# Moving one gate group, turning the first block's outputs on VectorE, and tying the stores of x to products

## The chip, the cores and the metric

The kernel runs on one NeuronCore of one Trainium2 chip. The metric is the device time of one execution in microseconds (us). Three executions of the kernel before took 2559.28, 2559.40 and 2559.43 us; their median is 2559.4 us. The trace comes from one more execution, which was recorded by the profiler.

## What is computed

The reference is one layer that mixes a short convolution (path A) with a chunked linear recurrence of eight heads (path B), for 2048 prompt tokens and 64 sample tokens, of width 1024:

```
h = rms_norm(x, g_pre);  vA, bA, cA, zA, q, f, iv, zB, gA, gB = split(h @ w_in)
yA = (silu(zA) * bA * conv3(cA * vA)) @ w_a_out
o  = hgrn2(q, k, v, logf)              # per head; chunks of 64 tokens, state 128x128
o  = o * rsqrt(mean(o*o) + eps)        # per head and token
o  = o * g_onorm
yB = (o * silu(zB)) @ w_b_out
merged = sigmoid(gA) * yA + sigmoid(gB) * yB
x  = x + rms_norm(merged @ w_o, g_post)
gate = sigmoid(rms_norm(x, g_ple) @ w_ple_gate)
x  = x + (p @ w_ple_proj) * gate
```

## The kernel before

**Layout.** Features lie on the 128 partitions and tokens along the free dimension. The 2112 tokens are cut into three blocks of 768, 704 and 640 tokens (`SIZES`, L36). Each block goes through path B's heads (`path_b`, L1213), path A (`path_a`, L880), the merge of both with the output projection (`in_turn`, L558), and a last stage with the final norm and the final gate (`final_norm` L1405, `final_gate` L1458).

**Products.** Each fp32 operand is split into a high part, which is rounded, and a low part, which is what rounding took away (`split`, L225: ScalarE writes the high part, VectorE the low one). A product is three passes, high by high, high by low and low by high (L442 to L444). Two column blocks of the weights and two halves of the block's tokens are taken together in `sgroup` (L427), which needs seven products instead of eight by adding and subtracting operands. I call this a group. One product of a group is 12 matmuls. The sums of the weights that a group needs (S1 to S4) and their low parts are made in the first block by VectorE and stored to DRAM (`keep_sum` L328, `split_w` L263); in later blocks they are loaded (L274, L236). Where a group was not done in the first block, its first run in a later block makes and stores the sums (`combined`, L341, with `first or i1 not in sums`). These stores go through the queue in `stores[0]`: SyncE's (SP) in the first block, GpSimd's (POOL) after it.

**Order of the work.** The kernel is written for a scheduler which orders each engine's instructions by dependencies and by the order of the program. `hook()` (L313) runs at the end of every product of a group and takes one entry of the list `hooks`; so side work is spread over products: one entry is one slot. `paced` (L300) adds a dependency of a DMA on the last matmul that was emitted so far (`last[0]`): the DMA is sent only when that matmul is done. `behind_all` and `tc.issue_after` only fix an order on an engine.

**Heads.** `head_prep` (L936) runs two groups for a head: f with v, then z with q (`sink_q`, L1019). The first block puts z through SiLU on ScalarE (L1023); the other blocks take a sigmoid (L1026) and multiply by v and by g_onorm on VectorE (L1027). `head_attn` (L1068) is the attention of a head over up to four pairs of chunks. Its last steps norm the output `on` (L1184) and then turn it, from tokens on partitions to features on partitions, so that it can be multiplied into z. In the first block TensorE turns it: six 128x128 transposes for each head (L1189), and VectorE multiplies the PSUM result by g_onorm and z (L1193, two instructions). In the other two blocks the pairs of chunks are turned in another way: VectorE transposes 32x32 blocks (`turned`, L1049, L1053), POOL stores the result to DRAM (`to`, L1055) and reads it back in another order (`in_rows`, L1057, L1060), and VectorE multiplies it into z (`scale_o`, L1209, L1211). Only the single chunk of 64 tokens that is left over goes through TensorE there (L1195). The finished z of each head is stored by POOL (`keep_z`, L1216, L1218).

**Gate groups.** The gates gA and gB are 16 column blocks, so 8 groups (`gates`, L868). The first block runs seven of them, one after each of heads 1 to 7. For the other two blocks `LEAD` = 7 groups run ahead, under the final norm of the block before (main loop); the eighth, columns 6 and 7 of gB, runs in `path_b` after the `head_prep` of head 5 (L1223, `hd == KH + 1`), with `stores[0]` set to SP meanwhile. The first block never makes the sums of this group, so the middle block makes them.

**The stores of x.** In the first two blocks the eight tiles of the new x (`xo`) are stored to DRAM in the last part of `final_norm` (L1447), and read back in `final_gate`. `fetch` (L1414) loads the eight tiles of the old x there. `final_norm` runs in hooks of the seven gate groups; in its last part, one step comes with every second product.

Of the kernel before, what the change touches and what calls it, by code (L numbers as in the profile page):

```python
# [14 lines left out]
ALU = mybir.AluOpType  # L15
# [3 lines left out]
P = 128  # L19
D = 1024  # L20
KB = D // P
KH = KB // 2
NH = 8
# [70 lines left out]
def hybrid_step(  # L94
# [17 lines left out]
    V, A, G, T, SP = nc.vector, nc.scalar, nc.gpsimd, nc.tensor, nc.sync  # L112
# [13 lines left out]
    def nm(s):  # L126
        uid[0] += 1
        return f"{s}_{uid[0]}"
# [38 lines left out]
    def spill(kind, j):  # L167
        return dram.tile([P, BN], F32, tag=f"{kind}{j}", name=nm(kind), bufs=2)[:, : width[0]]
# [13 lines left out]
    g_pre, g_on, g_post, g_ple = (vec[:, i, :] for i in range(4))  # L182
    cw = [vec[:, 4 + i, :] for i in range(3)]
    caus = [const.tile([P, P], I32, tag=f"caus{i}", name=f"caus{i}") for i in range(2)]
    keep = const.tile([P, BN], F32, tag="keep", name="keep")
# [53 lines left out]
    lows, turn, stores = {}, [0], [SP]  # L239
# [54 lines left out]
    last, hooks, copies, adds, ahead, evicted, freed, powers, means = [None], [], [None], [None], [], [], [], [], []  # L294
# [5 lines left out]
    def paced(dma):  # L300

        tc.add_manual_dep(
            dma.ins, last[0].name, mybir.DependencyInfo(mybir.DependencyClass.Sync, mybir.DependencyReason.DATA), reason="paced"
        )
# [170 lines left out]
    def half(t, h):  # L475
        return t[:, h * hn() : (h + 1) * hn()]

    def whole(x, y):

        if y is None:  # L480
            return x
        t = hf()
        freed[:] = [V.tensor_tensor(t, x, y, ALU.add).ins]
        return t
# [451 lines left out]
    def head_prep(bl, hc, hd, first, hs, before):  # L936
        n, npair = bl["n"], bl["npair"]
# [29 lines left out]
        ka, kb, qe, z = hf(npair * CH), rt(), rt(), rt()  # L967
# [51 lines left out]
        def sink_q(c, h, x, y):  # L1019
            if c == 1:  # L1020
                into(half(qe, h), x, y)
            elif first:
                A.activation(half(z, h), whole(x, y), AF.Silu)  # L1023
            else:
                v = whole(x, y)
                A.activation(half(z, h), v, AF.Sigmoid)  # L1026
                V.scalar_tensor_tensor(half(z, h), v, g_on[:, hd : hd + 1], half(z, h), ALU.mult, ALU.mult)  # L1027
# [4 lines left out]
            queries()  # L1032
        with behind_all([*wrote, *powers]):
            by_token = [in_rows("tv", npair)]
            if before is not None and before["on"] is not None:
                before["ot"] = in_rows("to", npair, before["on"])
            if not first:
                by_token.insert(0, in_rows("tk", npair))
# [29 lines left out]
    def head_attn(ip, gs, d, hd):  # L1068
# [3 lines left out]
        nt, ln = len(gs), gs[0]["len"]  # L1072
        o0, n = gs[0]["off"], nt * ln
        qe, z, att = d["qe"], d["z"], atts[ip]
        single = ln < P
# [26 lines left out]
        with placed():  # L1102
            for i, g in enumerate(gs):
                o = g["off"]
                shared = nt == 2 * SWAP
                if not single and (i < SWAP or not shared):
                    at = (d["more"] + 2 * i if shared else (o - SWAP * 2 * P) // P) * CH
# [26 lines left out]
        for i, g in enumerate(gs):  # L1134
            u = p_u[:, i * P : i * P + P]
            c = (g["off"] + ln) // CH - 1
# [25 lines left out]
        with placed():  # L1162
            for i, g in enumerate(gs):
                dst = p_o[:, i * P : i * P + P]
                T.matmul(dst, att[:, i, :], v[:, i], start=True, stop=prevs[i] is None)  # L1165
                if prevs[i] is not None:
                    T.matmul(dst, cols(d["qx"], g), prevs[i], start=False, stop=True)  # L1167
        if not d["first"] and not single:
            d["on"] = rt(d["npair"] * P) if d["on"] is None else d["on"]
            on = cols3(d["on"][:, o0:], nt)  # L1170
        else:
            on = tile3(2)
# [13 lines left out]
        p_t = ps_attn()  # L1186
# [1 line left out]
            for i in range(nt):  # L1188
                T.transpose(p_t[:, i * P : i * P + P], on[:, i, :], ident)  # L1189
        c = slice(o0, o0 + n)  # L1190
        turned_o = p_t[:, P - ln : P - ln + n]
        if d["first"]:
            V.scalar_tensor_tensor(z[:, c], turned_o, g_on[:, hd : hd + 1], z[:, c], ALU.mult, ALU.mult)  # L1193
        else:
            V.tensor_tensor(z[:, c], turned_o, z[:, c], ALU.mult)  # L1195
        yield

    def each(steps):
# [7 lines left out]
        if "ot" not in d:  # L1206
            d["ot"] = in_rows("to", d["npair"], d["on"])

    def scale_o(d, hd):  # L1209
        z = d["z"][:, : d["npair"] * P].rearrange("q (g i a) -> q g i a", i=4, a=32)  # L1210
        V.tensor_tensor(z, d["ot"], z, ALU.mult)  # L1211

    def path_b(bl, hc, first, kept, fills, hs, lead_sums=None):  # L1213


        def keep_z(hd, z):  # L1216
            kept["o", hd] = spill("o", hd)
            G.dma_start(kept["o", hd], z)  # L1218

        slots, base, d = {}, 0, None  # L1220
        for hd in range(NH):
            d = head_prep(bl, hc, hd, first, hs, d)
            if hd > 0 if first else hd == KH + 1:  # L1223
                queue, stores[0] = stores[0], SP
                next(fills, None)
                stores[0] = queue
            assert not hooks
            attn = [head_attn(i, gs, d, hd) for i, gs in enumerate(bl["parts"])]
            keep = partial(keep_z, hd, d["z"])
            piece = lead_sums and partial(next, lead_sums, None)  # L1230

            def at(slot, *steps):
                slots.setdefault(base + slot, []).extend(s if callable(s) else partial(next, s) for s in steps if s is not None)

            if first:
                late = int(hd == 0)
                for g in attn:
                    for slot in (1 + late, 4, 7, 10, 13):
                        at(slot + late + (g is attn[1]), g)
                at(15 + late, keep)  # L1240
                for slot in (15, 17, 19) if hd else (17,):
                    at(slot, piece)
                if hd == NH - 1:
                    for slot in range(22, 70, 4):
                        at(slot, piece)
            else:
                pairs, one = attn[:2], attn[2:]
                for slot, steps in enumerate((pairs[:1], pairs[1:], one, one, pairs, one, pairs, (), one)):
                    at(slot + 2, *steps)
                at(11, partial(turn_o, d))  # L1250
                at(14, partial(read_o, d))
                at(14 + 7, partial(scale_o, d, hd), keep)
            count = 14 + 7 * (first or hd + 1 == KH + 1) if hd + 1 < NH else 1 + max(slots) - base
            for slot in range(base, base + count):
                steps = slots.pop(slot, None)
                hooks.append(partial(each, steps) if steps else None)
            base += count
# [147 lines left out]
    def final_norm(bl, segs, xo, acc, h2, kept, ask_ahead=False):  # L1405

        c = slice(segs[0]["off"], segs[-1]["off"] + hn())
        n = len(segs) * hn()  # L1410
        acc2, rs, rs2 = rt(), rt(), rt()
        xks = []

        def fetch():  # L1414
            j = len(xks)
            if j < KB:
                xks.append(rt())
                G.dma_start(xks[j][:, c], x_fm[j * P : (j + 1) * P, segs[0]["t0"] : segs[0]["t0"] + n])

        for _ in range(2 if bl["last"] else 4):  # L1420
            fetch()
        if kept is not None:
            for j in range(KB):
                sum_squares(j, xo[j], acc, width[0])
                if j % 2:
                    yield
        yield from rms(acc, rs, segs, bl["last"])
        if ask_ahead:
            for _ in range(3):
                fetch()  # L1430
                fetch()
                yield
        for j in range(KB):
            fetch()
            xj = xo[j][:, c]
            V.scalar_tensor_tensor(xj, xj, g_post[:, j : j + 1], rs[:, c], ALU.mult, ALU.mult)
            V.tensor_tensor(xj, xj, xks[j][:, c], ALU.add)

            for i in (j,) if not bl["last"] else (j - 1,) if 0 < j < KB - 1 else (j - 1, j) if j else ():
                sum_squares(i, xo[i][:, c], acc2[:, c], n)  # L1440
            yield
        yield from rms(acc2, rs2, segs, bl["last"])
        ts = []
        for j in range(KB):
            if kept is not None:
                kept["x", j] = spill("x", j)
                G.dma_start(kept["x", j], xo[j])  # L1447
            if len(h2) <= j:
                h2.append((rt(dt=F32R), rt(dt=F32R)))

            for i in (j, j + 1) if j == 0 else (j + 1,):
                if i < KB:
                    ts.append(rt())
                    V.scalar_tensor_tensor(ts[i][:, c], xo[i][:, c], g_ple[:, i : i + 1], rs2[:, c], ALU.mult, ALU.mult)
            split(ts[j][:, c], h2[j][0][:, c], h2[j][1][:, c])
            yield
# [178 lines left out]
    fills = sized(blocks[0], gates(blocks[0], hc, kepts[0], True))  # L1635
    for bi, bl in enumerate(blocks):
        first, kept = bi == 0, kepts[bi]
# [26 lines left out]
        mg, xo, h2, acc = [], [], [], rt()  # L1664
# [17 lines left out]
        before, loads, ob, m = merge_in_turn(a, kept, mg, first)  # L1682
# [31 lines left out]
        if nxt:  # L1714
            xo.extend(stages[-1]["mid"])
            fills = sized(nxt, gates(nxt, hc, kepts[bi + 1], False))
# [65 lines left out]
```

## Time and profile before

| | |
|---|---|
| median of three executions | 2559.4 us |
| the profiled execution's own time | 2566.42 us |
| its span, first to last instruction | 2564.2 us |
| mean granted TensorE clock | 0.997 |
| TensorE matmul / weight load busy | 2533.4 / 2516.8 us |
| VectorE / ScalarE / POOL busy | 1795.1 / 1481.9 / 448.1 us |
| moved by DMA | 774.70 MB, mean 302 GB/s |

The profiled execution took 7.0 us more than the median. In the rows of the profile PE is TensorE, PEld its weight loads, DVE VectorE, ACT ScalarE, SP SyncE. A row of a group names the line, engine and operation, then output and inputs by the program's tile names with their sizes, how often (x), and after the bar the busy time and the mean ns of one, then the idle time ahead of it. A row of a window gives, for each engine, the busy us and in brackets how many instructions, then the granted TensorE clock as a share of full speed (PEclk), the busy share of the 16 DMA engines, and GB/s. Matmuls overlap, so the duration in their rows is longer than the distance from one to the next; the distance is what counts. A row of the timeline gives start, duration, instruction, and in square brackets the idle time ahead of it with what ended it.

### The profile page before, as it was taken

Reading aid. Unit: us, or ns where it says so; the run is one execution under the profiler, and the core shown is the slowest. Engines: PE = TensorE matmul, PEld = TensorE weight load, DVE = VectorE, ACT = ScalarE, POOL = GpSimd, SP = SyncE. Lnnn points to the kernel's source line nnn. Section 1 sums busy time; section 2 is a strip of 40 time slices with the busy share of each in tenths; the row PEclk is TensorE's granted clock in tenths of the full one; section 3 lists DMA queues with packets and bytes.
Section 4 is the critical chain, followed back from the end, with each engine's and each line's share of the span. In section 5 each row is a group of like instructions: output and inputs, shape, how many; then the busy total and the mean of one; then the engine's idle time right before and its main releaser. Section 6 shows DMA issues by size and latency. Waiting matters only on the chain. (4 is left out here: it accounts for less than half of the span.)

```text
span 2564.2 us, 47005 instructions
## 1 busy us (share of the span) xinstructions
PE 2533.4 (99%) x16070; PEld 2516.8 (98%) x16070; DVE 1795.1 (70%) x3549; ACT 1481.9 (58%) x2876; POOL 448.1 (17%) x793
## 2 busy tenths in 40 slices
PE   9999999999999999999999999999999999999999
PEld 9999999999999999999899999999999999999998
DVE  7888888898868775577574556887437766336967
ACT  6666666554453664466464555666446665446675
POOL 2011121230022021122122221102112221001011
PEclk9999999999999999999999999999999999999999
DMA  8789888998797888888888998998889999989986
GB/s 329 245 283 318 276 291 289 323 367 302 255 342 252 269 306 270 302 275 293 283 276 308 338 389 311 337 303 315 306 302 319 326 328 321 302 300 324 336 273 202
DMA packets 370399, 774.70 MB, mean 302 GB/s; under 512 B 45734, under 2 KB 50528, under 8 KB 370160
## 3 DMA queue, kind: packets, MB, share of 16 engines
q1 hardware_dynamic: 321840, 582.95, 66.8%
q0 software_dynamic: 48320, 188.75, 20.6%
q8 instruction: 126, 2.06, 0.3%
q14 instruction: 113, 0.93, 0.1%
HBM read 559.43 MB, written 212.10 MB: 301 GB/s over the span
## 5 line engine op out<-in xcount | busy, mean ns | idle before, releaser
L442 PE MATMUL pg<-r,hi 128*128 128x320 f32 (+2 forms) x3304 | 1082.3, 328 | 1.7 <-ACT hf L456 1.4
L443 PE MATMUL pg<-r,hi 128*128 128x320 f32 (+2 forms) x3304 | 1067.7, 323 | 0.0
L444 PE MATMUL pg<-r,lo 128*128 128x384 f32 (+2 forms) x2368 | 773.3, 327 | 10.6 <-DMA lo<-low 9.7
L273 ACT CAST hi<-raw 128x512 fp32r<-128x512 f32 x726 | 447.1, 619 | 498.4 <-PE pg L443 172.4
L442 PEld LDWEIGHTS pg<-r,hi 128*128 128x128 f32 x3304 | 623.4, 189 | 2.9 <-ACT hf L456 2.2
L443 PEld LDWEIGHTS pg<-r,hi 128*128 128x128 f32 x3304 | 623.1, 189 | 0.0
L444 PEld LDWEIGHTS pg<-r,lo 128*128 128x128 f32 x2368 | 445.6, 188 | 12.8 <-DMA lo<-low 11.5
L444 PE MATMUL pg<-r,s 128*128 128x320 f32 (+1 forms) x936 | 296.6, 317 | 3.0 <-DMA s<-low 3.0
L594 PE MATMUL pg<-r,hi 128*128 128x320 f32 (+2 forms) x864 | 277.2, 322 | 0.5 <-DVE r L226 0.4
L593 PE MATMUL pg<-r,hi 128*128 128x320 f32 (+2 forms) x864 | 274.9, 322 | 0.0
L226 ACT CAST hi<-raw 128x512 fp32r<-128x512 f32 x252 | 155.3, 620 | 157.8 <-PE pg L443 42.7
L226 DVE TENSOR_TENSOR r<-r,r 128x320 fp32r<-128x320 f32 (+7 forms) x350 | 206.3, 609 | 45.7 <-ACT r L226 44.2
L226 DVE TENSOR_TENSOR lo<-raw,hi 128x512 fp32r<-128x512 f32 x231 | 158.1, 687 | 80.5 <-ACT hi L226 76.3
L226 ACT CAST r<-r 128x320 fp32r<-128x320 f32 (+7 forms) x350 | 183.1, 556 | 43.8 <-DVE r L1333 8.4
L595 PE MATMUL pg<-r,lo 128*128 128x352 f32 (+2 forms) x564 | 181.0, 321 | 1.3 <-DMA lo<-low 1.2
L444 PEld LDWEIGHTS pg<-r,s 128*128 128x128 f32 x936 | 176.3, 188 | 4.0 <-DMA s<-low 3.9
L226 ACT CAST hi<-s 128x512 fp32r<-128x512 f32 x160 | 98.8, 618 | 137.6 <-PE pg L443 109.8
L632 PE MATMUL pg<-r,hi 128*128 128x384 f32 (+2 forms) x512 | 167.0, 327 | 0.2 <-DVE r L226 0.2
L631 PE MATMUL pg<-r,hi 128*128 128x384 f32 (+2 forms) x512 | 165.6, 327 | 0.2 <-ACT hi L273 0.2
L594 PEld LDWEIGHTS pg<-r,hi 128*128 128x128 f32 x864 | 162.2, 188 | 2.1 <-DVE r L226 1.6
L593 PEld LDWEIGHTS pg<-r,hi 128*128 128x128 f32 x864 | 161.2, 188 | 1.3 <-ACT r L226 0.8
L456 ACT COPY hf<-pg 128x352 f32<-128x352 f32 (+2 forms) x354 | 157.4, 446 | 2.6 <-PE pg L444 2.1
(394 smaller groups left out, 4109.6 us busy)
## 6 DMA issues: line engine op xcount, KB each, us to landing
raw<-w_blk SPq DMA_DIRECT2D x578, 256.0 KB, 4.4
raw<-S SPq DMA_DIRECT2D x440, 256.0 KB, 4.7
lo<-low SPq DMA_DIRECT2D x421, 256.0 KB, 4.4
s<-low SPq DMA_DIRECT2D x305, 256.0 KB, 4.6
low<-lo SPq DMA_DIRECT2D x275, 256.0 KB, 4.1
S<-s SPq DMA_DIRECT2D x156, 256.0 KB, 3.9
low<-r POOLq DMA_DIRECT2D x50, 256.0 KB, 5.2
r<-w_blk POOLq DMA_DIRECT2D x48, 256.0 KB, 7.1
```

Of the source, the lines that this page charges most:

```text
L226: return A.copy(hi, src).ins, V.tensor_tensor(lo, src, hi.bitcast(F32), ALU.subtract).ins
L273: A.copy(hi, raw)
L442: add(hi[:, k, :], xhi, start=start and k == 0, stop=False)
L443: add(hi[:, k, :], xlo, start=False, stop=False)
L444: last[0] = add(lo[:, k, :], xhi, start=False, stop=k == KH - 1).ins
L456: copied = A.copy(got[n], ps[bank])
L593: add(hi[:, k, :], xhi, start=start and k == 0, stop=False)
L594: add(hi[:, k, :], xlo, start=False, stop=False)
L595: last[0] = add(lo[:, k, :], xhi, start=False, stop=k == KH - 1).ins
L631: T.matmul(ps, hi[:, k % 4, :], xhi[:, c], start=k == ks[0], stop=False)
L632: T.matmul(ps, hi[:, k % 4, :], xlo[:, c], start=False, stop=False)
```

## The change

Five edits:

1. In the first block z is multiplied by g_onorm on ScalarE, right after SiLU (two instructions of 128x384 for each head).
2. The first block's outputs are turned as in the other blocks: VectorE, `to` and back, `scale_o`. The TensorE transposes and their two multiplies go. The turn is at slot 13 of the head's list, the read at 17, the multiply with the store of z at 24.
3. `scale_o` is tied to the last product that was emitted (`paced`), in all blocks.
4. In the middle block the eighth gate group runs ahead of head 0 instead of after head 5, its stores still on SP. In the last block it stays, with its stores on the queue of the rest. The list of head 4 in the middle block gets 14 slots instead of 21.
5. The stores of x are asked for one tile earlier in the program, and each is tied to the last product that was emitted.

```diff
             elif first:
                 A.activation(half(z, h), whole(x, y), AF.Silu)
+                A.mul(half(z, h), half(z, h), g_on[:, hd : hd + 1])
...
-        if not d["first"] and not single:
+        if not single:
             d["on"] = rt(d["npair"] * P) if d["on"] is None else d["on"]
...
-        turned_o = p_t[:, P - ln : P - ln + n]
-        if d["first"]:
-            V.scalar_tensor_tensor(z[:, c], turned_o, g_on[:, hd : hd + 1], z[:, c], ALU.mult, ALU.mult)
-        else:
-            V.tensor_tensor(z[:, c], turned_o, z[:, c], ALU.mult)
+        V.tensor_tensor(z[:, c], p_t[:, P - ln : P - ln + n], z[:, c], ALU.mult)
...
-        V.tensor_tensor(z, d["ot"], z, ALU.mult)
+        paced(V.tensor_tensor(z, d["ot"], z, ALU.mult))
...
+        late_gates = KH + 1 if bl["last"] else None
+        if not first and not bl["last"]:
+            queue, stores[0] = stores[0], SP
+            next(fills)
+            stores[0] = queue
         for hd in range(NH):
             d = head_prep(bl, hc, hd, first, hs, d)
-            if hd > 0 if first else hd == KH + 1:
-                queue, stores[0] = stores[0], SP
+            if hd > 0 if first else hd == late_gates:
                 next(fills, None)
-                stores[0] = queue
...
-                    for slot in (1 + late, 4, 7, 10, 13):
+                    for slot in (1 + late, 4, 7, 10):
                         at(slot + late + (g is attn[1]), g)
-                at(15 + late, keep)
+                at(13 + late, partial(turn_o, d))
+                at(17 + late, partial(read_o, d))
+                at(24 + late, partial(scale_o, d), keep)
...
         for j in range(KB):
-            if kept is not None:
-                kept["x", j] = spill("x", j)
-                G.dma_start(kept["x", j], xo[j])
+            for i in () if kept is None else (0, 1) if j == 0 else (j + 1,):
+                if i < KB:
+                    kept["x", i] = spill("x", i)
+                    paced(G.dma_start(kept["x", i], xo[i]))
```

More of the change, by code (lines that the diff above doesn't have):

```diff
@@ L1034, in head_prep @@
             by_token = [in_rows("tv", npair)]
-            if before is not None and before["on"] is not None:
+            if before is not None and not first:
                 before["ot"] = in_rows("to", npair, before["on"])
@@ L1207, in read_o, with scale_o @@
             d["ot"] = in_rows("to", d["npair"], d["on"])
-    def scale_o(d, hd):
+    def scale_o(d):
         z = d["z"][:, : d["npair"] * P].rearrange("q (g i a) -> q g i a", i=4, a=32)
-        V.tensor_tensor(z, d["ot"], z, ALU.mult)
+        paced(V.tensor_tensor(z, d["ot"], z, ALU.mult))
     def path_b(bl, hc, first, kept, fills, hs, lead_sums=None):
@@ L1251, in path_b @@
                 at(14, partial(read_o, d))
-                at(14 + 7, partial(scale_o, d, hd), keep)
-            count = 14 + 7 * (first or hd + 1 == KH + 1) if hd + 1 < NH else 1 + max(slots) - base
+                at(14 + 7, partial(scale_o, d), keep)
+            count = 14 + 7 * (first or hd + 1 == late_gates) if hd + 1 < NH else 1 + max(slots) - base
             for slot in range(base, base + count):
```

## The prediction

> **What bounds the kernel now.** First the page's head: TensorE is busy nearly all the time, so the time falls only where matmuls go or where TensorE's waits go.
>
> ```profile
> span 2564.2 us, 47005 instructions
> PE 2533.4 (99%) x16070; PEld 2516.8 (98%) x16070; DVE 1795.1 (70%) x3549; ACT 1481.9 (58%) x2876; POOL 448.1 (17%) x793
> ```
>
> Then the list of TensorE's waits. It is short, and headed by loaded weights, low parts and sums, that land late (total, times, longest). For a split by VectorE it waited once in the whole span.
>
> ```profile
> PE pg L444 <- DMA lo<-low: 9.7, 4, 6.0
> ```
> ```profile
> PE pg L444 <- DMA s<-low: 3.0, 3, 1.3
> ```
> ```profile
> PE pg L444 <- DVE lo L226: 0.8, 1, 0.8
> ```
>
> The timeline puts the longest in the middle block, in the gate group behind head 5. TensorE stops for 6.03 us, and afterwards the granted clock is halved: the windows hold 9, 17 and then 27 matmuls in 4 us.
>
> ```profile
> 1263.38 0.66 PE L444 MATMUL pg<-r,lo 128*128 128x352 f32 x1 [6.03 <-DMA lo<-low]
> ```
> ```profile
> 1262.00:1266.00 4.00, 2.62 (x9) 2.63 (x10) 0.00 (x0) 0.00 (x0) 0.00 (x0) 0.50 0.99 333
> 1266.00:1270.00 4.00, 4.00 (x17) 4.00 (x16) 0.01 (x1) 1.11 (x3) 0.00 (x0) 0.56 0.78 267
> 1270.00:1274.00 4.00, 4.00 (x27) 4.00 (x26) 1.04 (x2) 2.68 (x5) 1.11 (x2) 1.00 0.76 257
> ```
>
> The load was late because it was sent late. SP sends in order; it stood from 1255.4 to 1260.77, and the load followed at 1261.66.
>
> ```profile
> 1254.68 0.72 SPq L274 DMA_DIRECT2D lo<-low  x1
> 1260.77 0.32 SPq L274 DMA_DIRECT2D s<-low  x1
> ```
> ```profile
> 1261.66 0.50 SPq L274 DMA_DIRECT2D lo<-low  x1
> ```
>
> What it stood for is VectorE: this group makes its sums anew. VectorE first waited for a head's turned output (L1211), then worked through the head's queries, and split the sum s that SP's next loads wait for only at 1259.53.
>
> ```profile
> 1255.77 0.82 DVE L1211 TENSOR_TENSOR r<-r,r 128x640 f32<-128x640 f32 x1 [1.11 <-DMA r<-to]
> ```
> ```profile
> 1259.53 0.68 DVE L226 TENSOR_TENSOR lo<-s,hi 128x512 fp32r<-128x512 f32 x1
> ```
>
> The second place is the final norm of the first block. Two waits (4.00 - 2.95 and 4.00 - 1.50 us) and a stretch of lowered clock follow a stretch at 410 GB/s.
>
> ```profile
> 926.00:930.00 4.00, 2.95 (x19) 2.67 (x18) 2.04 (x4) 2.10 (x3) 0.00 (x0) 1.00 1.05 410
> 930.00:934.00 4.00, 1.50 (x9) 1.21 (x8) 2.27 (x3) 2.56 (x5) 0.63 (x2) 1.00 0.72 259
> 934.00:938.00 4.00, 4.00 (x19) 4.00 (x18) 2.73 (x4) 2.79 (x5) 1.00 (x2) 0.63 1.01 365
> 938.00:942.00 4.00, 4.00 (x25) 4.00 (x24) 2.82 (x5) 1.24 (x2) 0.00 (x0) 0.95 1.00 319
> ```
>
> The eight stores of x run just there, from the first to the last:
>
> ```profile
> 910.80 0.54 POOL L1447 DMA_DIRECT2D x<-r  x1 [3.14 <-DVE r L1437]
> ```
> ```profile
> 942.72 0.54 POOL L1447 DMA_DIRECT2D x<-r  x1 [5.51 <-DVE r L1437]
> ```
>
> **The change part by part.** The sum is made in the profiled execution (2566.42 us: the span and 2.2 us around it).
>
> **Transposes.** 48 TensorE transposes go (8 heads, six each).
>
> ```profile
> 332.42 0.60 PE L1189 MATMUL pa<-ident,r 128*128 128x128 f32 x4
> 332.78 0.42 PE L442 MATMUL pg<-r,hi 128*128 128x384 f32 x1
> 333.04 0.34 PE L443 MATMUL pg<-r,hi 128*128 128x384 f32 x1
> 333.22 0.34 PE L444 MATMUL pg<-r,lo 128*128 128x384 f32 x1
> ```
>
> Four of them and the matmul behind take 333.04 - 332.42 = 0.62 us; a matmul alone takes 333.22 - 333.04 = 0.18. So one costs 0.11 us, and 48 cost **5.3 us**, all on TensorE. To gain it the rest must keep up. For each head VectorE loses two multiplies and gets a block transpose and a full multiply; ScalarE gets two scalings, whose nearest row is SiLU at the same size from SBUF.
>
> ```profile
> L1193 DVE SCALAR_TENSOR_TENSOR r<-pa,vec,r 128x512 f32<-128x512 f32 x8 | 6.0, 745 | 0.0
> ```
> ```profile
> L1193 DVE SCALAR_TENSOR_TENSOR r<-pa,vec,r 128x256 f32<-128x256 f32 x8 | 3.8, 478 | 0.0
> ```
> ```profile
> L1053 DVE STREAM_TRANSPOSE r<-r 128x768 f32<-128x768 f32 x8 | 12.6, 1580 | 0.0
> ```
> ```profile
> L1017 DVE TENSOR_TENSOR r<-r,qc 128x768 f32<-128x768 f32 x8 | 7.6, 952 | 0.0
> ```
> ```profile
> L1023 ACT ACTIVATE r<-hf 128x384 f32<-128x384 f32 x8 | 4.2, 527 | 18.4 <-DVE hf L483 18.4
> ```
>
> That is 1.58 + 0.95 - 0.75 - 0.48 = +1.31 us on VectorE and 2 x 0.53 = +1.05 on ScalarE for each head. A head of about 52 us has room on both, and the tightest stretch that I found in it, at head 4, has the split done at 338.98 and its first matmul at 341.83, 2.85 us later:
>
> ```profile
> 234.00:286.00 52.00, 52.00 (x323) 51.86 (x322) 45.66 (x90) 34.17 (x69) 8.45 (x14) 1.00 0.87 305
> 492.00:543.00 51.00, 51.00 (x294) 51.00 (x293) 48.30 (x88) 30.22 (x64) 15.48 (x27) 1.00 1.01 367
> 543.00:594.00 51.00, 50.23 (x287) 49.92 (x286) 44.28 (x79) 24.95 (x52) 11.67 (x22) 1.00 0.99 361
> ```
> ```profile
> 338.30 0.68 DVE L226 TENSOR_TENSOR lo<-raw,hi 128x512 fp32r<-128x512 f32 x1
> ```
> ```profile
> 341.83 0.34 PE L444 MATMUL pg<-r,lo 128*128 128x384 f32 x1
> ```
>
> The block transpose stands ahead of such splits; with one scaling it delays them by at most 1.58 + 0.53 = 2.11 us, under 2.85, and the multiplies that go stood in the same stretch. The new multiply stands a group later, behind the eviction (L462) that waits for the same product, so its tie adds no wait; the read-back has seven products, some 15 us. POOL's queue gets a store and a read for each head; the next head's values are read behind them and used eleven products later. So the heads cost nothing new. Their tail does: in the second and third window above the DMA engines are full and VectorE is busy for 48.30 of 51 us, and there VectorE already waits 4.58 us for a store to leave a buffer. TensorE loses 0.77 us in that window.
>
> ```profile
> 547.73 0.69 DVE L226 TENSOR_TENSOR lo<-s,hi 128x512 fp32r<-128x512 f32 x1 [4.58 <-DMA low<-lo]
> ```
>
> Head 7 brings two more transfers of 393 KB into it, 2.1 us at 367 GB/s, and 1.31 us of VectorE. Bounds: 0 if they slip through, 3.4 if all of it reaches TensorE (and 1.5 for a halved clock). I take **+1.5**. A page of the Trainium skill speaks against this part: "VectorE: DVE Perf Modes", Rules for kernel authors, gives a full 128x128 transpose to TensorE where a PSUM result will do. The rows say it costs 0.11 us of the engine that bounds and the other way 1.31 us a head of one that does not; by the rule this part would bring 0 instead of 5.3.
>
> **Gate group.** The stop goes with its cause, if the group does not stop in its new place: 6.03 us, and the clock's share, with 0.148 us for a matmul (4.00 / 27): 2.62 / 0.148 - 9 = 8.7 and 27 - 17 = 10 matmuls too few, 2.8 us. Together **-8.8**. The new place is the end of the final gate, where today head 0's first group makes its sums:
>
> ```profile
> 1057.00:1070.00 13.00, 12.87 (x80) 12.58 (x79) 5.63 (x11) 6.88 (x12) 1.63 (x3) 1.00 0.99 344
> ```
>
> There TensorE loses 0.13 us and VectorE is busy for 5.63 of 13 us, so SP's stores of sums will find them made. Behind those stores stand the loads for head 0. Bounds: 0.1 as today, 8.8 if the stop moves along. I take **+0.5**.
>
> **Stores of x.** What follows the burst is 1.05 + 2.50 us of waits and 8 + 2 matmuls too few, 1.5 us: **-5.0**. The stores now go one by one, with the last 15 or so of the 49 products; behind them on POOL stand gate stores and the reloads for the final gate, which has its first merge some 10 us later. In their new stretches move today:
>
> ```profile
> 961.00:990.00 29.00, 29.00 (x181) 29.00 (x180) 22.65 (x33) 18.81 (x33) 3.78 (x7) 1.00 0.78 252
> 1798.00:1824.00 26.00, 26.00 (x179) 26.00 (x178) 20.15 (x31) 19.17 (x36) 2.88 (x6) 1.00 0.93 309
> ```
>
> Eight tiles of 393 KB make 252 + 108 = 360 GB/s, and in the next block eight of 360 KB 309 + 111 = 420. The trace has moved 410 (926:930). So the first fits, I take +0.5; the second is 10 to 20 GB/s over, at most 0.5 MB or 1.3 us, I take all of it. Bounds 0 and 5.0, the old price. Net **-3.2**.
>
> **scale_o in the other blocks.** It now stands 16 instructions later on VectorE, where its data has landed. That saves VectorE waits of this kind:
>
> ```profile
> DVE r L1211 <- DMA r<-to: 44.7, 16, 8.7
> ```
>
> TensorE waits for none of them except in the gate group counted above: 0. If the tied matmul were late, the state updates behind it would be; bounds -1 to +1.
>
> **Sum:** -5.3 + 1.5 - 8.8 + 0.5 - 3.2 = -15.3, so 2551.1 us for a profiled execution. The one before was 7.0 us over its median. If that excess sits in the waits that go, the median after is 2551.1; if it is spread evenly, 2544.1. I take the middle, rounded: **2547**, own range 2541 to 2553.
>
> **Rivals.**
> *The stores saturate their new stretches.* For it: the rate above is at what the trace has reached. Against: 410 GB/s did run. It brings back the 5.0 of the burst instead of 1.8 new: 2550. The Trainium skill ("DMA: Bandwidth & Descriptors", Where 436 GB/s comes from) puts the limit of a core at about 358 GB/s. By it 2 and 62 GB/s are over, an estimate of 1.7 MB or 4.7 us; the rows at 365 and 410 GB/s speak against it, for short stretches.
> *The stop moves with the group.* Same sums, same SP queue, and a halved clock behind it; against it VectorE's 5.63 of 13. It costs 8.8 - 0.5: 2555.
> *VectorE becomes the bound in the first block's heads (slower).* It decides if more than 5.0 of its 6.34 idle us in a head (52.00 - 45.66) are waits that nothing can fill; then 1.31 more do not fit and the lead of 2.85 us is gone after two heads. For the other six: 1.31 longer than today, 0.66 of transposes not gained, and 1.5 for a halved clock, as in 934:942, together 3.5 a head or 21 us: 2568. Against it: one wait for a split in the whole span.
>
> **How the numbers follow.** Forecast 0.60, stores 0.14, stop moves 0.15, VectorE 0.09, other 0.02. A measurement can tell about 0.2%, 5.1 us, from no change: 2554.3 to 2564.5. Faster takes the first two and a third of the third, 0.79; same 0.12; slower 0.09. The range reaches from 2540 (all new costs nil, excess spread evenly) to 2558 (stop moves and the tail costs 4.9), and leaves out the slower rival.
>
> **What would show it.** Right: no rows of L1189 in the first block's heads, and each of these about 0.6 us shorter; no stop over 2 us in the middle block's heads; windows at 926 to 942 with 27 matmuls in 4 us; x stores one each 3.9 us. Wrong: VectorE or its splits among TensorE's releasers in the heads, a stop near 550, at the start of the middle block, or at 1798 to 1824.

## The result, and the profile after

The changed kernel takes 2550.36 us (median of 7 executions, 2547.27 to 2554.84) against 2559.28 us for the kernel before (7 executions): ratio 0.9967, with a 95% interval of 0.9955 to 0.9978. That is 8.9 us faster, about 0.35%. The forecast was 2547 us, the range 2540 to 2558. The head of the page after:

```profile
span 2549.3 us, 46960 instructions
PE 2526.8 (99%) x16022; PEld 2511.3 (99%) x16022; DVE 1803.4 (71%) x3549; ACT 1487.5 (58%) x2892; POOL 458.6 (18%) x809
```

The list of TensorE's waits after (total, times, longest):

```profile
PE pg L444 <- DVE lo L226: 5.0, 5, 1.5
...
PE pg L444 <- DMA s<-low: 2.0, 1, 2.0
PE pg L444 <- DMA lo<-low: 1.3, 2, 1.0
```

Set it beside the list of before: the waits for loaded low parts (`lo<-low`) fell from 9.7 us to 1.3, and the longest from 6.0 to 1.0. At the head stands now what stood there once, a split by VectorE that is late: 0.8 us became 5.0. The prediction named that as a sign that a step of it is wrong.

The windows over the final norm of the first block (lined up with the trace of before, this stretch begins 2 us later there and ends 3 us earlier):

```profile
923.00:927.00 4.00, 4.00 (x27) 4.00 (x26) 4.00 (x6) 2.10 (x4) 0.00 (x0) 1.00 1.04 376
927.00:931.00 4.00, 4.00 (x27) 4.00 (x26) 4.00 (x7) 3.60 (x7) 0.54 (x1) 1.00 0.62 183
931.00:935.00 4.00, 4.00 (x27) 4.00 (x26) 3.00 (x5) 2.74 (x6) 0.54 (x1) 1.00 0.89 297
935.00:939.00 4.00, 4.00 (x27) 4.00 (x26) 3.83 (x5) 1.35 (x3) 0.00 (x0) 1.00 0.91 287
```

27 matmuls in each, as the prediction asked: the waits and the lowered clock are gone. And the two stretches into which the stores of x moved. The second lies 17 us earlier in this trace than in that of before, so the third row shows it at its place: the eight stores of the middle block leave from 1781.45 to 1802.49 us.

```profile
961.00:990.00 29.00, 29.00 (x179) 29.00 (x178) 20.39 (x30) 16.71 (x29) 5.93 (x11) 1.00 0.99 360
1798.00:1824.00 26.00, 26.00 (x168) 26.00 (x167) 8.51 (x13) 10.66 (x20) 4.83 (x9) 1.00 0.96 363
1781.00:1807.00 26.00, 26.00 (x178) 26.00 (x177) 20.48 (x31) 19.13 (x36) 6.38 (x12) 1.00 1.02 376
```

TensorE is busy for all of the three.

To see where the time went I lined up the traces by TensorE's product matmuls, 14,616 in each, and noted at every sixtieth how far the second kernel is ahead or behind. The kernel before was traced a second time for this (run before_again, below), since its first trace was 7.0 us over the median and the second was not. From that trace to the one after:

| stretch of the kernel | us | term in the prediction |
|---|---|---|
| first block's heads and their tail, to 572 us | +4.4 | -5.3 + 1.5 |
| from there to 887 us | +0.4 | |
| final norm of the first block, 887 to 943 us | -4.7 | -5.0 + 0.5 |
| end of the final gate, start of the middle block | +1.4 | +0.5 |
| gate group of the middle block | -8.3 | -8.8 |
| near 1375 us | -1.7 | 0 (scale_o) |
| near 1470 us | -0.9 | 0 |
| from there to 1730 us | +1.6 | 0 |
| final norm of the middle block, 1730 to 1790 us | -2.0 | 0 |
| all that comes later | +1.1 | +1.3 |
| sum (spans 2557.9 and 2549.3 us) | -8.7 | -15.3 |

The +1.6 us are almost all one wait for a low part of a sum (`s<-low`, 2.0 us at 1716.42); why it is late was not sought. The -2.0 us lie where the middle block's stores of x ran before.

### The profile page after: what moved, and what is told of

Read it like the earlier page. It is cut to its first block, busy times and chain, and to the rows that moved or that the text cites. A ratio compares the mean times of both kernels' runs of the same rounds, so it can differ in the third digit from the quotient of the medians.

```text
span 2549.3 us, 46960 instructions
## 1 busy us (share of the span) xinstructions
PE 2526.8 (99%) x16022; PEld 2511.3 (99%) x16022; DVE 1803.4 (71%) x3549; ACT 1487.5 (58%) x2892; POOL 458.6 (18%) x809
## 4 chain that ended last, share of the span: by engine, by line
PE 89%; DMA 4%; issue 3%; DVE 2%; POOL 1%; ACT 0%; SPq 0%; DVEq 0%; POOLq 0%; ACTq 0%
PE pg L442 19%; PE pg L444 19%; PE pg L443 19%; PE pg L593 5%; PE pg L594 5%; PE pg L595 5%; PE pg L632 3%; PE pg L633 3%; PE pg L631 3%; DMA lo<-low 2%; PE pa L1126 1%; PE pa L1166 1%; PE pa L1168 1%; PE pa L1112 1%; PE pa L1111 1%
```

## The experiments

The times of a row and of the kernel before, to which its ratio is, come from one chip. The first row is the result above.

| run | what it is | median us | ratio to before, 95% interval |
|---|---|---|---|
| changed kernel | | 2550.4 | 0.9967 (0.9955 to 0.9978) |
| before_again | kernel before | 2559.6 | 1.0001 (0.9991 to 1.0012) |
| no_turn | changed, edits 1 and 2 undone | 2546.1 | 0.9948 (0.9936 to 0.9961) |
| old_gates | changed, edit 4 undone | 2559.2 | 1.0002 (0.9993 to 1.0011) |
| old_stores | changed, edit 5 undone | 2555.0 | 0.9981 (0.9972 to 0.9989) |
| untied_scale | changed, edit 3 undone after the first block | 2553.0 | 0.9971 (0.9959 to 0.9982) |
| loads_first | changed, read of `to` behind weight loads | 2547.4 | 0.9951 (0.9938 to 0.9965) |
| last_by_pe | changed, head 7 turned by TensorE | 2542.4 | 0.9947 (0.9933 to 0.9960) |
| both_cures | the last two together | 2542.9 | 0.9940 (0.9928 to 0.9952) |
| last_by_pe_vector | last_by_pe and VectorE's work | 2549.1 | 0.9954 (0.9940 to 0.9968) |
| last_by_pe_transfers | last_by_pe and the transfers | 2544.2 | 0.9940 (0.9928 to 0.9952) |
| old_gates_low_elsewhere | old_gates, other buffers for low parts | 2557.9 | 0.9992 (0.9981 to 1.0003) |
| old_gates_loads_ahead | old_gates, its loads ahead on SP | 2560.2 | 1.0000 (0.9990 to 1.0010) |

An interval is some 3 us to either side. Differences under 4 us between two of these kernels are not told by the times, only by the place in the trace.

**before_again.** No edit.

> The kernel before, unchanged, traced once more. Theory 1 (the one of the prediction: SP's in-order queue makes the middle block's gate group stop in every execution): the trace shows a stop of 5 to 7 us of TensorE near 1263 us again, and its span is again about 7 us over the median of the timed runs. Theory 2 (the stop's size is a matter of chance, and the traced execution was one of the slower ones): a stop of under 3 us there, and a span at the median, about 2557 to 2558 us.

```profile
PE pg L444 <- DMA lo<-low: 9.8, 4, 6.0
```

The stop of 6.0 us is there again, and the span is at the median, 2557.9 us. So each theory is half right: the stop belongs to this kernel, and the 7.0 us by which its first trace was long were for the most part elsewhere. Lined up, the two traces of the same kernel part in many small steps, 6.3 us in all, only 1.25 us of them at the stop and 0.9 at the final norm of the first block.

**no_turn, old_gates, old_stores, untied_scale** each undo one part (the edits are shortened, with notes in brackets):

```
no_turn:       first block turned by T.transpose again; no A.mul on z
old_gates:     -        late_gates = KH + 1 if bl["last"] else None
               -        if not first and not bl["last"]: (next(fills) ahead of the heads)
               +            if hd > 0 if first else hd == KH + 1: (next(fills) behind head 5)
old_stores:    -    paced(G.dma_start(kept["x", i], xo[i]))      (j + 1)
               +    G.dma_start(kept["x", j], xo[j])             (j)
untied_scale:  -    paced(V.tensor_tensor(z, d["ot"], z, ALU.mult))
               +    V.tensor_tensor(z, d["ot"], z, ALU.mult)     (tied in the first block alone)
```

> The changed kernel with the first block's outputs turned by TensorE again (edits 1 and 2 undone), the other edits kept. Theory 1 (prediction: the turn brings 5.3 us of transposes and costs 1.5): slower than the changed kernel by 3.8 us, about 2554.2 us. Theory 2 (the trace after: from the first head to the end of the first block's heads and their tail the changed kernel lost 3.8 us against before, in spite of the transposes that went): faster than the changed kernel by 3 to 5 us, about 2546.5 us.

> The changed kernel with the middle block's late gate group back behind head 5 (edit 4 undone). Theory 1 (the stop is there in every execution and costs 8.8 us, the new place 0.5): 8.3 us slower than the changed kernel, about 2558.7 us, and its trace shows a stop of over 5 us in the group. Theory 2 (the tie of scale_o, edit 3, already takes away VectorE's wait for the turned output, which held up the sums; or the stop is smaller in most executions): 1 to 4 us slower, about 2552 to 2554 us, with a stop of under 3 us.

> The changed kernel with the stores of x untied, and in the program where they were (edit 5 undone). Theory 1 (prediction: the burst costs 5.0 us, the new places 1.8): 3.2 us slower than the changed kernel, about 2553.6 us, with waits of TensorE for loaded weights between 926 and 942 us. Theory 2 (the trace after shows 5.6 us gained between 910 and 950 us and nothing lost between 961 and 990 or 1798 and 1824 us): 5 to 6 us slower, about 2556 us.

> The changed kernel with scale_o tied to a product in the first block alone, as before in the other two (edit 3 undone there). The prediction's term: 0, bounds -1 to +1: 2549.4 to 2551.4 us. Rival (the waits near 1381 and 1475 us, 3.2 us in the trace of before and not in that after, went because of this tie): 2552 to 2554 us, with waits of TensorE over 1 us near these places again.

Without the turn the kernel is 4.3 us faster (4.9 by the ratios): theory 2. With the gate group in its old place all of the gain is gone, 8.9 us, and its trace shows the old stop, although VectorE no longer waits for the turned output:

```profile
PE pg L444 <- DMA lo<-low: 6.2, 1, 6.2
```

So theory 1 has the size right; whether it has the cause comes below. With the old stores 4.7 us are lost (3.6 by the ratios, which the times alone hardly tell from nothing), between both theories, and the trace has the wait for a low part back at its place:

```profile
933.85 0.43 PE L444 MATMUL pg<-r,lo 128*128 128x352 f32 x1 [2.15 <-DMA lo<-low]
```

Lined up with the changed kernel, 2.3 us of the loss lie there, and another 2.4 between 1760 and 1780 us, where the middle block's stores of x run again as one burst:

```profile
1760.00:1765.00 5.00, 3.67 (x23) 3.15 (x22) 1.22 (x2) 2.49 (x6) 0.00 (x0) 1.00 1.01 368
```

The tie of scale_o can't be told from nothing by the time (2.6 us by the medians, 1.0 by the ratios). But one wait goes with it. In the timelines of before_again and of untied_scale TensorE waits near the same product, in all traced kernels with the tie it doesn't:

```profile
1374.98 0.43 PE L442 MATMUL pg<-r,hi 128*128 128x352 f32 x1 [1.40 <-ACT hf L456]
```
```profile
1363.43 0.43 PE L442 MATMUL pg<-r,hi 128*128 128x352 f32 x1 [0.70 <-ACT hf L456]
```

**Where the turn loses: loads_first, last_by_pe, both_cures.** Two places cost the changed kernel time that no_turn does not lose: 3.8 us near 340 us, in head 4 (the expectation below has 4.4), and 6.2 us between 527 and 580 us, behind head 7. At the first, TensorE's waits make up 1.8 us; behind them the granted clock is 0.77 from 340 to 345 us and 0.89 from 345 to 350. For its cause look at POOL's queue. In no_turn:

```profile
326.51 0.81 POOL L1060 DMA_DIRECT2D r<-tv  x1
327.32 2.15 POOL L379 DMA_DIRECT2D r<-w_blk  x4
```

In the changed kernel, which is almost 4 us ahead at this point:

```profile
329.54 0.77 POOL L1061 DMA_DIRECT2D r<-to  x1 [3.16 <-DMA to<-r]
330.31 0.76 POOL L1061 DMA_DIRECT2D r<-tv  x1
331.05 1.62 POOL L379 DMA_DIRECT2D r<-w_blk  x3
333.96 0.55 POOL L379 DMA_DIRECT2D r<-w_blk  x1 [1.29 <-issue]
```

The read of `to` waits 3.16 us for its own store to land, and four loads of weights, which the sums made ahead need, stand behind it. ScalarE then waits for them, with the rounding for TensorE's next products (`hi`) behind:

```profile
339.91 0.62 ACT L226 CAST r<-r 128x512 fp32r<-128x512 f32 x1 [3.67 <-DMA r<-w_blk]
...
340.81 0.62 ACT L226 CAST hi<-raw 128x512 fp32r<-128x512 f32 x1
```

loads_first changes that order (and asks for the read three slots later), last_by_pe takes head 7 off the new way:

```diff
 loads_first:
-                G.dma_start(t, w_blk[i, h])
+                asked.append(G.dma_start(t, w_blk[i, h]).ins)
...
-            d["ot"] = in_rows("to", d["npair"], d["on"])
+            with behind_all(asked[-4:] if d["first"] else ()):
+                d["ot"] = in_rows("to", d["npair"], d["on"])
...
-                at(17 + late, partial(read_o, d))
+                at(20 + late, partial(read_o, d))
 last_by_pe:
-        if not single:
+        if not single and d["by_dram"]:
...
+            d["by_dram"] = not first or hd + 1 < NH
...
+                else:
+                    for g in attn:
+                        at(13 + (g is attn[1]), g)
+                    at(15, keep)
```

> The changed kernel; in the first block's heads the read of the turned output is put behind the four loads of weights for the sums made ahead (r<-w_blk, L379) in POOL's queue. The changed kernel's trace loses 4.4 us near 340 us, in head 4, against the kernel whose outputs TensorE turns. Theory 3 (queue order: the read stands in POOL's in-order queue until its own store has landed, 3.2 us, and holds back the loads behind it, for which ScalarE then waits in front of the splits): the stop near 340 us is gone, 4.4 us faster than the changed kernel, about 2546 us. Rival (the loads are late because the DMA engines have more to move): the stop stays, under 1 us of gain, 2549.5 to 2550.5 us.

> The changed kernel; the last head of the first block alone is turned by TensorE again, as before (six transposes, no store to DRAM and read). Theory 4 (the tail: in the stretch from 527 to 580 us the DMA engines are full, and head 7's two transfers of 393 KB make the stores of low parts land later, so VectorE's splits wait for their buffers and TensorE for the splits; 6.2 us in the trace): 6.2 - 0.65 = 5.6 us faster than the changed kernel, about 2544.8 us, with no wait of TensorE for a split between 527 and 580 us. Rival (the tail loses what the earlier heads left behind, stores and gates that are late, not what head 7 adds): under 2 us of gain, 2548.5 to 2550.5 us.

> The two edits of loads_first and last_by_pe together. If theories 3 and 4 hold, seven heads gain 0.65 us each over the kernel whose outputs TensorE turns in all heads (2546.1 us) and lose nothing: about 2541.5 us, which would be below all kernels so far. If one of the two losses has another cause, 2545 us or more.

loads_first: TensorE's waits from 325 to 345 us are down to one, of 0.5 us; lined up with the changed kernel it gains 3.0 us there, and 3.0 us in the median (4.1 by the ratios). Theory 3 holds, with a size of 3.0 instead of 4.4. It is more than one lucky trace: against no_turn the nine traces in which head 4 goes over DRAM in the old order lose 2.2 to 4.3 us at this place, the two with the new order (loads_first, both_cures) 0.7 to 0.8. So the loss varies from one trace to the next.

```profile
PE pg L444 <- DVE lo L226: 0.5, 1, 0.5
```

last_by_pe: no wait of TensorE is left between 525 and 580 us. The windows of the changed kernel and of last_by_pe over that stretch (280 matmuls against 316):

```profile
525.00:580.00 55.00, 50.36 (x280) 48.34 (x280) 47.81 (x88) 28.21 (x62) 16.05 (x27) 1.00 0.99 364
```
```profile
525.00:580.00 55.00, 55.00 (x316) 55.00 (x316) 51.39 (x93) 32.10 (x68) 15.47 (x29) 1.00 1.02 376
```

Lined up it gains 5.7 us, as expected (6.3 in that stretch, less 0.6 for the transposes of head 7 ahead of it). Again the other traces agree: between 527 and 580 us the seven in which head 7 goes over DRAM lose 4.4 to 8.8 us against no_turn, the four in which it does not lose 0.0. The medians give 7.9 us, the ratios 5.1; two of its five executions took 2548.1 and 2550.4, the others 2541.6 to 2542.4. both_cures is the fastest traced, with a span of 2537.6 us, and by its ratio beats the changed kernel (0.9940, interval to 0.9952, against 0.9967 from 0.9955), some 6.9 us. That the two together beat last_by_pe or no_turn is not shown by the times.

**What in the tail costs: last_by_pe_vector, last_by_pe_transfers.** Each adds one half of head 7's way to last_by_pe, on tiles that nobody uses:

```diff
 last_by_pe_vector:
+                    at(13, partial(spare_turn, d))     # block transpose of 128x768
+                    at(24, partial(spare_scale, d))    # multiply of 128x768
 last_by_pe_transfers:
+                    at(13, partial(spare_store, d))    # 393 KB to DRAM
+                    at(17, partial(spare_read, d))     # and back
```

> The kernel last_by_pe (last head of the first block turned by TensorE) with VectorE's part of the turn added as work that nobody uses: one block transpose and one multiply of 128x768 at the same slots, and no transfers. Theory 4a (the transfers make the tail late, not VectorE's work): as last_by_pe, 2542 to 2545 us, no waits of TensorE for splits over 1 us between 527 and 580 us. Rival 4b (VectorE's 2.5 us of additional work make it late): as the changed kernel, 2549 to 2551 us.

> The kernel last_by_pe with only the transfers of the turn added: a tile of 393 KB stored to DRAM at slot 13 and read back at slot 17, used by nobody. Theory 4a (the transfers): as the changed kernel, 2548 to 2551 us, with waits of TensorE for splits between 527 and 580 us of 4 us or more in all. Rival 4b (VectorE's work): as last_by_pe, 2542 to 2545 us.

These did not decide between the theories. By time last_by_pe_vector looks like rival 4b, but in its trace TensorE is busy for all 55.00 us from 525 to 580, so VectorE's half alone costs the tail nothing; its extra time is spread over five places far from there, and by the ratios it differs from last_by_pe by 1.8 us with an uncertainty of about 5. last_by_pe_transfers loses nothing in the tail either, but it failed to put the question: its source was ready earlier, so its read left at 459.94 us, where the changed kernel's leaves at 484.94. What the changed kernel's queue shows there is the pattern of head 4 once more, with the wait for VectorE's turn added:

```profile
480.68 0.54 POOL L1056 DMA_DIRECT2D to<-r  x1 [1.80 <-DVE r L1054]
484.94 0.77 POOL L1061 DMA_DIRECT2D r<-to  x1 [3.72 <-DMA to<-r]
485.70 2.12 POOL L751 DMA_DIRECT2D r<-x_tok  x4
...
488.00 1.61 POOL L379 DMA_DIRECT2D r<-w_blk  x3
491.75 0.54 POOL L379 DMA_DIRECT2D r<-w_blk  x1 [2.14 <-DMA r<-to]
```

In last_by_pe the same eight loads leave from 476.44 us on:

```profile
476.44 2.13 POOL L751 DMA_DIRECT2D r<-x_tok  x4
478.56 0.55 POOL L889 COPY r<-hist_p 128x2 f32<-128x2 f32 x1
479.06 2.13 POOL L379 DMA_DIRECT2D r<-w_blk  x4
```

So 2 MB of loads come 9 us later (some 7 by TensorE's products, which last_by_pe has 2.4 us earlier there), among stores of low parts for whose buffers VectorE then waits. A store sent at 492.5 us lands after 9.6 us, at 502.05, and with that VectorE goes on; one sent at 493.1 us in last_by_pe takes 5.1 (the lists of DMA issues: KB, us to landing):

```profile
low<-lo SPq DMA_DIRECT2D x1, 256.0 KB, 9.6
```
```profile
low<-lo SPq DMA_DIRECT2D x1, 256.0 KB, 5.1
```
```profile
502.18 0.69 DVE L226 TENSOR_TENSOR lo<-s,hi 128x512 fp32r<-128x512 f32 x1 [3.70 <-DMA low<-lo]
```

From 480 to 505 us VectorE waits 6.9 us for such stores, in last_by_pe 0.6. There too the eight loads are followed by late stores, up to 10.0 us for those sent from 479 to 482 us, and VectorE hardly waits for them; why it has to in the changed kernel is not settled. TensorE's waits for VectorE's splits come 30 us later, from 534 us on. That head 7's way over DRAM costs the tail is shown; that it does so through POOL's queue is read from the trace and not tested by itself, nor is the sum of both halves without it.

**Why the gate group stops: old_gates_low_elsewhere, old_gates_loads_ahead.** In old_gates SP still stood, 6.2 us, but for another reason than the prediction's: a load into a buffer of tile s waited for the store of a sum to land. The list of SP's waits of the kernel before has the same, as the second row shows: its store of a sum was sent at 1252.53 us and landed at 1260.75, and SP went on at 1260.77. The prediction read this wait as VectorE's.

```profile
SPq L274 <- DMA S<-s: 6.2, 1, 6.2
```
```profile
SPq L274 <- DMA S<-s: 5.3, 1, 5.3
```

Two edits tried to take this wait away:

```diff
 old_gates_low_elsewhere, in low_tile:
+        plain[0] -= 1
-        if turn[0] % 7 in (1, 3, 5):
+        if turn[0] % 7 in (1, 3, 5) and plain[0] < 0:
 old_gates_loads_ahead, in split_w:
+            left[0] -= 1
-            SP.dma_start(lo.bitcast(F32), lows[key])
+            with behind_all(wanted if left[0] >= 0 else ()):
+                ins = SP.dma_start(lo.bitcast(F32), lows[key]).ins
```

> The kernel old_gates (gate group of the middle block behind head 5), in which the seven low parts that are loaded after this group take buffers of the tile lo alone, and none of the three of tile s, from which the group's sums are still being stored. In the trace of old_gates a store of a sum, sent at 1245.16 us, lands 9.2 us later, and SP's next load into an s buffer leaves at 1254.37, 1.7 us after VectorE's last split of a sum is done. Theory 5 (SP stands because the store must land before its buffer is free): the stop of 6.2 us falls to under 2 us, and the time by 6 to 9 us, to 2550 to 2553 us. Rival (theory 1 as the prediction put it: VectorE's splits of the sums are late, and hold up SP's queue): the stop stays over 4 us, 2556 to 2560 us.

> The kernel old_gates (gate group of the middle block behind head 5); the low parts for the next group are loaded by SP only behind the two loads that the gate group itself still waits for (lo<-low, of its blocks A12 and A22), and not ahead of them as in old_gates. Theory 5 (a load for a later group waits in SP's in-order queue for a store of a sum to land, and the gate group's own loads stand behind it): the stop falls from 6.2 us to under 2, and the time by 6 to 9 us against old_gates, to 2550 to 2553 us. Rival (theory 1 as the prediction put it: VectorE's late splits of the sums hold the group up): the stop stays over 4 us, 2556 to 2560 us.

The stop stayed at 6.2 us in both, and so did the time. In the first the wait stayed too, 5.6 us: the scheduler filled the free buffers with low parts of a still later group. In the second the group's loads did go ahead, SP's wait for these stores fell to 2.4 us, and nothing was gained. Theory 5 falls with that. Here is what both it and theory 1 overlooked: the load that ends the stop was sent long before. The list of DMA issues of the kernel before, for 1254.5 to 1255.2 us (its load leaves at 1254.68 us, lands at 1263.33, and TensorE goes on at 1263.38), then for 1234 to 1247 us:

```profile
lo<-low SPq DMA_DIRECT2D x1, 256.0 KB, 8.7
```
```profile
lo<-low SPq DMA_DIRECT2D x1, 256.0 KB, 3.7
```

It is the same in the other two traces: in old_gates a load sent at 1247.35 us lands 8.7 us later and the stop ends at 1256.11, in old_gates_loads_ahead one sent at 1251.84 lands 8.7 us later and the stop ends at 1260.55.

A load that took 3.7 us to land some 20 us earlier takes 8.7. TensorE stopped at 1257.35 us, so with 3.7 us the stop would have been some 1 us (an estimate from these rows). Ahead of it, between 1249.5 and 1254.7 us, twelve transfers were sent, 3.4 MB in 5.1 us, where the fastest 4 us window that was read (414 GB/s) would make 2.1 MB; the windows themselves moved 216 GB/s from 1250 to 1254 us and 310 from 1254 to 1258:

```profile
low<-lo SPq DMA_DIRECT2D x3, 256.0 KB, 7.3
raw<-S SPq DMA_DIRECT2D x2, 256.0 KB, 7.6
tk<-r POOLq DMA_DIRECT2D x1, 320.0 KB, 2.8
r<-to POOLq DMA_DIRECT2D x1, 320.0 KB, 5.7
r<-tv POOLq DMA_DIRECT2D x1, 320.0 KB, 7.1
r<-tk POOLq DMA_DIRECT2D x1, 320.0 KB, 8.0
s<-low SPq DMA_DIRECT2D x1, 256.0 KB, 6.8
S<-s SPq DMA_DIRECT2D x1, 256.0 KB, 8.2
lo<-low SPq DMA_DIRECT2D x1, 256.0 KB, 8.7
```

The group's stores and loads leave together with a head's store and three reads of turned tiles. In the new place, ahead of head 0, there are none of these. In the changed kernel's list from 1049 to 1059 us loads of this kind take 4.5 us, and TensorE waits 1.0 us for one of them, at 1061.09:

```profile
S<-s POOLq DMA_DIRECT2D x3, 256.0 KB, 5.0
lo<-low SPq DMA_DIRECT2D x3, 256.0 KB, 4.5
```

That the pile of transfers makes the load late is read from these lists; whether the head's reads or the group's own stores weigh more was not tried.

## Why the prediction was right, and where it was wrong

The sign and the range held, and two large terms were of the right size. One part went the other way, and the start of the sum was mis-chosen. That the time lies 3.4 us from the forecast is in part luck: the sum of -15.3 us is 6.6 us more than what was gained between two traces at the median (-8.7), and the part of the first trace's excess that the forecast kept hid some 3 us of that.

1. **Transposes (-5.3 + 1.5): wrong.** The 5.3 us are real: lined up, each of the first heads gains 0.57 to 0.65 us. But the part as a whole costs 4.3 us (no_turn). The step that failed is "So the heads cost nothing new", and in it the sentence on POOL's queue, which counted "a store and a read for each head" and asked only about the next head's values. The read waits for its store to land, in order, and the loads of weights behind it are late: 3.8 us in head 4, of which 3.0 came back with another order. The tail was seen as a risk and mis-sized, 6.2 us against 1.5 taken and 4.9 as the upper bound: I counted the two transfers and VectorE's 1.31 us, not the eight loads held up behind the read. What the prediction cited from the Trainium skill ("VectorE: DVE Perf Modes", Rules for kernel authors), that a full transpose belongs on TensorE where a PSUM result will do, came out right here, though VectorE's own time was not shown to be the reason.
2. **Gate group (-8.8 + 0.5): right in size, wrong in cause.** Measured: -8.3, +1.4 at the new place, 8.9 for the whole by old_gates. The step that failed is "The load was late because it was sent late": the load sent at 1261.66 us lands only after the stop. The right one left at 1254.68 us and was 8.7 us under way. SP's own wait was misread too, as above. Moving the group was the right cure for the wrong reason; the one edit that did shorten SP's wait gained nothing.
3. **Stores of x (-5.0 + 0.5 + 1.3): right in sign and about in size.** -4.7 us at the burst from before_again (2.3 came back in old_stores), nothing lost in the new stretches. The middle block's burst was put at nothing: there the traces gain 2.0 us, and old_stores loses 2.4. The burst is a pile of the same kind: the load that TensorE waited for at 933 us was sent at 920.08 us, in the kernel before, and landed 13.3 us later; the one load of the same kind that the changed kernel sends from 917 to 924 us takes 5.3.

```profile
lo<-low SPq DMA_DIRECT2D x1, 256.0 KB, 13.3
```
```profile
lo<-low SPq DMA_DIRECT2D x1, 256.0 KB, 5.3
```

4. **scale_o (0, bounds -1 to +1):** outside its bounds by a little. 1.7 us were gained near 1375 us, where TensorE's wait comes and goes with the tie; 1.0 came back in untied_scale.
5. **The starting point.** The prediction took the middle of two readings of the first trace's excess of 7.0 us. before_again decides for the most part: of the 6.3 us between the two traces only 2.2 were at the places where the change removes waits. By the other reading alone, 2544.1, the forecast would have been 6 us too low; the hedge of 3 us hid about half of that.

The rivals: the stores did not saturate their new stretches; the stop did not move, but for a wait of 1.0 us; VectorE did not become the bound of the heads, but its late splits did appear, for the reason in point 1.

## What to carry to other kernels

When a wait for a load ends a stop, find out when that load was sent before asking why it was late: time of issue plus time to landing must give the end of the stop. On POOL's queue a store followed by a read of the same data held up everything behind it until the store had landed, 3.2 and 3.7 us here; look at what is queued there, not only at what the pair itself moves. And where a change has several parts, undo each one alone: here one of three cost half of what another brought.

## What the runs showed of the hardware

- In these rows the landing time goes with what SP and POOL sent in the few us before: a load of 256 KB took 3.7, 5.3, 8.7 and 13.3 us.
- The stretches from 961 to 990 and from 1798 to 1824 us ran at 360 and 363 GB/s, that from 1781 to 1807 us at 376, without a wait of TensorE. The Trainium skill ("DMA: Bandwidth & Descriptors", Where 436 GB/s comes from) gives about 358 GB/s as a core's limit at HBM; these long stretches sit just above it. The Trainium skill ("Perfetto Trace Analysis", Roofline) says that this is a core's share when both cores of a pair are active, and that a single core can pull more, up to about 435 GB/s; the windows agree with that. Single windows of 4 us were above it: 410 in the prediction's rows, 414 in old_stores from 934 to 938 us.
- Waits on VectorE of 6.9 us, from 480 to 505 us, show up on TensorE only from 534 us on, by the reading above. The wait and its cause can be far apart in the timeline.
